# A hybrid decoder step on one core: the input projection with TensorE's order written out and the attention heads cut into smaller steps

## The chip, the cores and the metric

One core of a Trainium2 chip runs the whole kernel as one program. The metric is the device time of one execution in microseconds (us). TensorE (PE in the profile), VectorE (DVE), ScalarE (ACT), GpSimd (POOL) and the queue that issues most transfers (SP) work at the same time and wait for each other through semaphores. Each of them takes its instructions in the order that was laid down when the kernel was built.

## The reference, cut to what matters

```python
h = rms_norm(x, norm_mix_pre)                  # 1024 prompt rows + 8 sample rows, width 1024
rq, rk, rv, rg, dq, dk, dv = split(h @ w_in)   # 28 column blocks of 128
ro = retention_prompt(rq, rk, rv)              # 4 retention heads, chunks of 128 rows
# 4 differential heads; per block of 128 query rows and map m = 0, 1:
s[m] = dq[m] @ dk[m].T * 64**-0.5 + alibi      # causal
p[m] = softmax(s[m])
do = (p[0] - lam * p[1]) @ dv
# the 8 sample rows attend to 1024 cached keys each: 64 key pages and 64 value pages of 128 x 512
x = x + rms_norm(concat(retention_out(ro, rg), subnorm(do)) @ w_o)
x = x + rms_norm(conv_ffn(rms_norm(x)))        # gated MLP, width 2816
```

Everything is float32. The large products are made from three float32r products of high and low parts (`prod3`).

## The kernel before, in words

**Blocks.** The input projection makes 28 column blocks of 128 outputs, each transposed, in three segments of 344 of the 1032 rows. A segment is 24 products (8 slices of the width, three products each, L114 to L116), and a block is 72. VectorE scales each finished segment out of PSUM (`z_evac`, L220), and splits the next block's weights into high and low (L109, after ScalarE's L108). Blocks 20 and 24 are made in front of the loop; the loop then walks `blocks_left`, numbered n = 0 to 25: first block 16, then nine more blocks for the differential heads (e >= 16), then sixteen for the retention heads.

**Side work.** Three generators are advanced from inside this loop, one `next` at a time, and each `yield` ends one step. `sides` runs the four differential heads and then the four retention heads. `credit` grows by a rate after every segment, and each whole credit runs one step: `D_RATE` 1.42 while differential blocks are made, `R_RATE` 0.88 afterwards. A third generator, `sample_attention`, starts behind block 19 and is paced by `K_PACE` 3.0 and `V_PACE` 2.35 steps a segment: one step takes one cached page. A key page is multiplied on GpSimd (L493) and summed on VectorE (L484); of the value pages every second one goes to GpSimd (L577, L579), the others to VectorE (L584, L586). Pages have four buffers (`PG_BUFS`).

**A differential head** (`diff_head`) splits its queries and keys into high and low parts and moves halves between partitions by nine transfers on SP's queue (L324 to L332), loads the position bias, and turns its values by 8 transposes. For each of 8 blocks of 128 query rows ("rows" below, i = 0 to 7, width 128(i+1)) it makes scores for two maps (L345, L346), adds the bias and finds the minimum on VectorE (L348), takes the exponential on ScalarE (L400), joins the two maps on VectorE (L408, L409), transposes the joined weights (`tr`, L292), copies them on ScalarE (L357) and multiplies them with the values (`av_mm`, L366). `tr` and `av_mm` of row i come while row i+2 is being scored. A float32 product such as L366 is issued as two instructions. The weights live in eight buffers shared by all such tiles (`aux`).

**What sets the order.** A planner orders every engine's instructions when the kernel is built, by its own costs, with the order of the program as priority. It may put a head's products far in front of block products that stand earlier in the program. Only in the MLP (`fixed`) is TensorE held to the order of the program.

Of the kernel before, what the change touches and what calls it, by code (L numbers as in the profile page):

```python
# [9 lines left out]
F32 = mybir.dt.float32  # L10
# [3 lines left out]
ALU = mybir.AluOpType  # L14
# [31 lines left out]
D_RATE, R_RATE, K_PACE, V_PACE = 1.42, 0.88, 3.0, 2.35  # L46
# [5 lines left out]
def step_kernel(ctx: ExitStack, tc: tile.TileContext, gam, g128, xT, w_in, w_o, w_f, w_y, norms, ngb, cst, subln,  # L52
# [257 lines left out]
    def diff_head(h):  # L310
        zq, zk, zv = Z.pop(16 + h), Z.pop(20 + h), Z.pop(24 + h)
# [7 lines left out]
        ql = zq[:, 0:T].bitcast(F32R)  # L319
        nc.scalar.activation(qs[0], zq[:, 0:T], AF.Copy)  # L320
        nc.scalar.activation(ks[0], zk[:, 0:T], AF.Copy)
        nc.vector.tensor_tensor(ql, zq[:, 0:T], qs[0].bitcast(F32), ALU.subtract)
        nc.vector.tensor_tensor(kl[0], zk[:, 0:T], ks[0].bitcast(F32), ALU.subtract)
        nc.sync.dma_start(ks[1][lo_h].bitcast(F32), ks[0][hi_h].bitcast(F32))  # L324
        nc.sync.dma_start(ks[1][hi_h].bitcast(F32), ks[0][hi_h].bitcast(F32))
        nc.sync.dma_start(qs[1][hi_h].bitcast(F32), qs[0][hi_h].bitcast(F32))
        nc.sync.dma_start(qs[1][lo_h].bitcast(F32), ql[hi_h].bitcast(F32))
        nc.sync.dma_start(ks[0][hi_h].bitcast(F32), ks[0][lo_h].bitcast(F32))
        nc.sync.dma_start(qs[0][hi_h].bitcast(F32), ql[lo_h].bitcast(F32))
        nc.sync.dma_start(kl[1][lo_h].bitcast(F32), kl[0][hi_h].bitcast(F32))  # L330
        nc.sync.dma_start(kl[1][hi_h].bitcast(F32), kl[0][hi_h].bitcast(F32))
        nc.sync.dma_start(kl[0][hi_h].bitcast(F32), kl[0][lo_h].bitcast(F32))  # L332
# [3 lines left out]
        yield  # L336
# [4 lines left out]
        def score(i, m, n0, w, pt, mn):  # L341
            n1 = min(w, n0 + 512)
            sps = bank("S", "sps")[:, 0:n1 - n0]
            q = slice(i * P, (i + 1) * P)
            nc.tensor.matmul(sps, lhsT=qs[m][:, q], rhs=ks[m][:, n0:n1], start=True, stop=False)  # L345
            nc.tensor.matmul(sps, lhsT=qs[m][:, q], rhs=kl[m][:, n0:n1], start=False, stop=True)  # L346
            mo = pa.tile([P, 1], F32, tag="mn", bufs=6, name="mn")
            nc.vector.tensor_tensor_reduce(pt[:, n0:n1], sps, bias[:, 1024 - w + n0:1024 - w + n1],  # L348
                                           -1.0, mn, ALU.add, ALU.min, mo)
            return mo  # L350
# [30 lines left out]
        on0 = None  # L381
        mt = m_out("mtd")
        for i in range(8):
            w = (i + 1) * P
            if i > 1:
                tr(i - 2)
# [16 lines left out]
            p0, p1 = pm_  # L403
# [7 lines left out]
            yield  # L411
            if i == 6:
                post2(0, on0)
        tr(6)
        av_mm(6)
        yield
        tr(7)
        av_mm(7)
        on1 = post1(1)
        yield  # L420
        yield
        post2(1, on1)
# [180 lines left out]
    def ret_head(h):  # L603
# [8 lines left out]
        for g in range(2):  # L612
            aps = bank4("S", "aps")
            for i in range(4):
# [3 lines left out]
                                    ALU.mult)  # L618

        for g in range(2):  # L620
            transpose4(blocks(zv, g), lambda tp: nc.scalar.activation(vn[:, 4 * g:4 * g + 4, :], tp, AF.Copy))
        yield
        for g in range(2):
            transpose4(blocks(zk, g), lambda tp: nc.scalar.activation(
                kn[:, 4 * g:4 * g + 4, :], tp, AF.Identity, scale=ct[:, C_KD + h:C_KD + h + 1]))
        nc.gpsimd.tensor_tensor(qd, qd, rd[:, 1:2, :].broadcast_to([P, 8, P]), ALU.mult)
        yield
        st = aux([P, 8, P], name="st")
        for g in range(2):
# [4 lines left out]
            for i in range(4):  # L634
# [3 lines left out]
                else:  # L638
                    nc.vector.scalar_tensor_tensor(st[:, c, :], st[:, c - 1, :], g128[h], kvp[:, i, :],
                                                   ALU.mult, ALU.add)  # L640
        nc.scalar.dma_start(rsp[h], st[:, 7, :])
# [766 lines left out]
```

## Time and profile before

| | |
|---|---|
| median of 3 runs | 1392.24 us (1391.69 to 1393.86) |
| the profiled execution: time, span | 1392.55 us, 1390.8 us |
| PE busy | 1316.7 us (95%) |
| DVE busy | 977.7 us (70%) |
| ACT busy | 573.9 us (41%) |
| POOL busy | 491.7 us (35%) |
| mean granted clock of TensorE | 0.987 of 2.4 GHz |

The time of an execution is 1.75 us more than the span, which runs from the first to the last instruction. Busy times are shares of the span. A matmul's busy time is modelled and overlaps with the next one's, so a stretch in which products follow each other closely shows as fully busy; how fast products really go is read from the distance between their starts.

### The profile page before, as it was taken

How to read it: one execution, taken by the hardware profiler on the slowest of the kernel's cores; microseconds unless marked ns; L12 is line 12 of the kernel's file. 1: busy time of each engine (PE TensorE's matmuls, PEld its weight loads, DVE VectorE, ACT ScalarE, POOL GpSimd, SP SyncE). 2: the span in 40 equal slices, each digit the busy share in tenths (PEclk: the TensorE clock that was granted, in tenths of full speed). 3: DMA queues.
4: the chain of work that ended last, by engine and by line, in shares of the span. 5: the costliest groups of instructions: out<-in, count | busy, mean ns of one | idle time of the engine just before them, and what ended most of it. 6: DMA issues, size and time to landing. Idle time of an engine off the chain costs nothing.

```text
span 1390.8 us, 22794 instructions
## 1 busy us (share of the span) xinstructions
PE 1316.7 (95%) x8235; PEld 1269.2 (91%) x8235; DVE 977.7 (70%) x1773; ACT 573.9 (41%) x1148; POOL 491.7 (35%) x402
## 2 busy tenths in 40 slices
PE   6999989889999999996799999999999999989998
PEld 5999887878999998996799999999999999989976
DVE  6575759879678865477877777767777655576585
ACT  5254515235222144343444434344444435546544
POOL 5300456745546621438523313323323100050130
PEclk9999999999999999998999999999999999999999
DMA  5434285764554534231122222221221268668675
GB/s 220 127 101 126 86 245 185 214 205 125 164 192 144 176 111 160 90 127 52 68 76 77 94 87 71 82 82 65 83 81 66 95 224 270 214 210 260 198 237 161
DMA packets 98355, 196.51 MB, mean 141 GB/s; under 512 B 17595, under 2 KB 47419, under 8 KB 98243
## 3 DMA queue, kind: packets, MB, share of 16 engines
q1 hardware_dynamic: 91378, 183.45, 41.6%
q10 hardware_dynamic: 6864, 11.62, 2.3%
q8 instruction: 64, 1.05, 0.3%
q14 instruction: 49, 0.39, 0.1%
HBM read 155.11 MB, written 30.48 MB: 133 GB/s over the span
## 4 chain that ended last, share of the span: by engine, by line
PE 64%; DVE 15%; POOL 7%; DMA 6%; issue 5%; ACT 2%; SPq 1%; POOLq 0%; DVEq 0%; ACTq 0%
PE ps_in L114 4%; PE ps_in L115 4%; PE ps_in L116 4%; PE ps_y L1218 3%; PE ps_y L1217 3%; PE ps_y L1219 3%; DVE acc_v L586 3%; PE pb L1023 3%; PE pb L1024 3%; PE pb L1022 3%; PE gp L1022 2%; PE up L1024 2%; PE pc L1023 2%; PE pc L1024 2%; PE up L1023 2%
## 5 line engine op out<-in xcount | busy, mean ns | idle before, releaser
L114 PE MATMUL ps_in<-xh,wh 128*128 128x344 f32 x672 | 223.6, 333 | 8.0 <-ACT xh L192 6.1
L115 PE MATMUL ps_in<-xl,wh 128*128 128x344 f32 x672 | 220.1, 328 | 2.1 <-DVE xl L193 2.1
L116 PE MATMUL ps_in<-xh,wl 128*128 128x344 f32 x672 | 218.6, 325 | 1.0 <-DVE wl L109 1.0
L114 PEld LDWEIGHTS ps_in<-xh,wh 128*128 128x128 f32 x672 | 129.0, 192 | 11.4 <-ACT xh L192 6.1
L160 POOL TENSOR_TENSOR acc<-acc,sq 128x344 f32<-128x344 f32 (+1 forms) x56 | 61.3, 1095 | 205.6 <-ACT sq L159 201.0
L115 PEld LDWEIGHTS ps_in<-xl,wh 128*128 128x128 f32 x672 | 128.9, 192 | 4.8 <-DVE xl L193 3.8
L1158 DVE TENSOR_TENSOR wyl<-wyraw,wyh 128x1024 fp32r<-128x1024 f32 x66 | 84.4, 1279 | 67.0 <-ACT wyh L1157 64.7
L116 PEld LDWEIGHTS ps_in<-xh,wl 128*128 128x128 f32 x672 | 128.9, 192 | 1.5 <-DVE wl L109 1.3
L1041 POOL TENSOR_TENSOR S<-wraw 128x512 f32<-128x512 f32 x20 | 30.8, 1541 | 266.5 <-DMA wraw<-in_w_f 239.3
L1218 PE MATMUL ps_y<-al,wyh 128*128 128x388 f32 x352 | 119.4, 339 | 2.4 <-DVE al L1169 2.4
L1219 PE MATMUL ps_y<-ah,wyl 128*128 128x388 f32 x352 | 119.1, 338 | 1.2 <-DVE wyl L1158 1.2
L1217 PE MATMUL ps_y<-ah,wyh 128*128 128x388 f32 x352 | 119.7, 340 | 0.3 <-ACT wyh L1157 0.3
L493 POOL TENSOR_TENSOR pg<-pg,qb 128x512 f32<-128x512 f32 x64 | 90.6, 1434 | 40.7 <-DMA pg<-in_kpool 26.6
L1157 ACT ACTIVATE wyh<-wyraw 128x1024 fp32r<-128x1024 f32 x66 | 69.7, 1056 | 59.5 <-PE ps_y L1218 33.1
L990 DVE TENSOR_TENSOR ww<-S,ww 128x512 fp32r<-128x512 f32 x80 | 85.4, 1086 | 8.4 <-ACT ww L989 8.4
L990 DVE TENSOR_TENSOR ww<-wraw,ww 128x512 fp32r<-128x512 f32 x80 | 74.8, 935 | 21.5 <-ACT ww L989 19.8
L989 ACT ACTIVATE ww<-wraw 128x512 fp32r<-128x512 f32 x80 | 50.2, 628 | 95.8 <-PE up L1024 65.5
L989 ACT ACTIVATE ww<-S 128x512 fp32r<-128x512 f32 x80 | 50.5, 634 | 94.1 <-POOL S L1042 35.0
L1169 DVE TENSOR_TENSOR al<-ar,ah 128x388 fp32r<-128x388 f32 (+2 forms) x110 | 62.5, 578 | 25.5 <-ACT ah L1168 24.7
L108 ACT ACTIVATE wh<-wraw 128x1024 fp32r<-128x1024 f32 (+1 forms) x41 | 42.5, 1036 | 83.3 <-PE ps_in L115 38.6
L1023 PE MATMUL pb<-tw,ww 128*128 128x344 f32 x240 | 76.8, 320 | 0.0
L1024 PE MATMUL pb<-tw,ww 128*128 128x344 f32 x240 | 76.8, 320 | 0.0
(324 smaller groups left out, 3877.6 us busy)
## 6 DMA issues: line engine op xcount, KB each, us to landing
wyraw<-in_w_y SPq DMA_DIRECT2D x66, 512.0 KB, 4.0
wraw<-in_w_f SPq DMA_DIRECT2D x44, 512.0 KB, 3.3
pg<-in_kpool SPq DMA_DIRECT2D x64, 256.0 KB, 3.0
pg<-in_vpool SPq DMA_DIRECT2D x64, 256.0 KB, 2.8
wraw<-in_w_in SPq DMA_DIRECT2D x27, 512.0 KB, 4.2
ar<-ad SPq DMA_DIRECT2D x44, 194.0 KB, 3.9
ad<-cc SPq DMA_DIRECT2D x20, 344.0 KB, 2.2
ar<-ad SPq DMA_DIRECT2D x44, 150.0 KB, 3.4
```

What stands on the lines that cost most here:

```text
L114: nc.tensor.matmul(ps, lhsT=wh[:, k, :], rhs=ah[:, k, n0:n1], start=(first and i == 0), stop=False)
L115: nc.tensor.matmul(ps, lhsT=wh[:, k, :], rhs=al[:, k, n0:n1], start=False, stop=False)
L116: nc.tensor.matmul(ps, lhsT=wl[:, k, :], rhs=ah[:, k, n0:n1], start=False, stop=(last and i == len(order) - 1))
L493: nc.gpsimd.tensor_tensor(kp, kp, qb.rearrange("p (a b) -> p a b", b=P), ALU.mult)
L989: nc.scalar.activation(hi, t, AF.Copy)
L990: nc.vector.tensor_tensor(lo, t, hi.bitcast(F32), ALU.subtract)
L1023: nc.tensor.matmul(ps, lhsT=w[:, 0, k], rhs=bl, start=False, stop=False, skip_group_check=True)
L1024: nc.tensor.matmul(ps, lhsT=w[:, 1, k], rhs=bh, start=False, stop=(last and k == 3), skip_group_check=True)
L1158: nc.vector.tensor_tensor(wl, raw, wh.bitcast(F32), ALU.subtract)
L1217: nc.tensor.matmul(pss[d], lhsT=wh[:, i, w], rhs=ah, start=(f == 0), stop=False)
L1218: nc.tensor.matmul(pss[d], lhsT=wh[:, i, w], rhs=al, start=False, stop=False)
L1219: nc.tensor.matmul(pss[d], lhsT=wl[:, i, w], rhs=ah, start=False, stop=(f == NF - 1))
```

## The change

From n = 1 on, TensorE's instructions keep the order of the program (`inorder`, closed behind the loop). Each segment's 24 products are cut into pieces of 9, 9 and 6, and side work is advanced (`tick`) behind each piece and not only behind each segment: nine times a block. The rates are given anew for the finer beat, with a third one, `E_RATE`, for retention blocks made while a differential head still runs. A differential head now yields after each map's scores, after each row's value products and after each row's transposes; value products come three rows behind the scores, a row further than their transposes' two. The splitting of a head's queries and keys (`diff_prep`) is taken out and run for the next head behind the current one's last scores. Retention heads yield in the middle of their first steps. Blocks 22 and 26 are made in front of block 19, so that sample attention, which starts behind block 19, starts at n = 7 and not at n = 5.

```diff
-D_RATE, R_RATE, K_PACE, V_PACE = 1.42, 0.88, 3.0, 2.35
+D_RATE, E_RATE, R_RATE, K_PACE, V_PACE = 1.6, 0.85, 0.55, 1.1, 0.85
...
+    def diff_prep(h):
+        zq, zk = Z.pop(16 + h), Z.pop(20 + h)
...
     def diff_head(h):
+        if h not in ready:
+            diff_prep(h)
+            for _ in range(16):
+                yield
+        ks, qs, kl, bias = ready.pop(h)
+        zv = Z.pop(24 + h)
         vn = zv[:, 0:T].rearrange("p (a b) -> p a b", b=P)
         for g in range(2):
             transpose4(blocks(zv, g), lambda tp: nc.scalar.activation(vn[:, 4 * g:4 * g + 4, :], tp, AF.Copy))
-        yield
+            yield
...
+        def done_row(i):
+            av_mm(i)
+            return post1(i // 4) if i % 4 == 3 else None
...
         for i in range(8):
             w = (i + 1) * P
-            if i > 1:
-                tr(i - 2)
...
             for m in range(2):
                 pt = aux([P, 1024], name="pt")
-                mn = score(i, m, 0, w, pt, 3e38)
-                if m == 1 and i > 1:
-                    av_mm(i - 2)
-                    if i == 5:
-                        on0 = post1(0)
-                if w > 512:
-                    mn = score(i, m, 512, w, pt, mn)
+                mn = score(i, m, w, pt)
                 nc.scalar.activation(pt[:, 0:w], pt[:, 0:w], AF.Exp, bias=mn, scale=-1.0,
                                      accum_out=sm[:, m:m + 1])
                 pm_.append(pt)
+                yield
+                if m == 0:
+                    if i > 2:
+                        on = done_row(i - 3) or on
+                        yield
+                    if i > 1:
+                        tr(i - 2)
+                        yield
...
+        if h < H - 1 and have(17 + h, 21 + h):
+            diff_prep(h + 1)
+        av_mm(5)
+        yield
+        tr(6)
+        yield
+        post2(0, on)
+        yield
+        tr(7)
+        yield
+        av_mm(6)
+        yield
+        on = done_row(7)
+        for _ in range(4):
             yield
...
-    blocks_left = [16, 17, 21, 25, 18, 19, 22, 26, 23, 27] + \
+    blocks_left = [16, 17, 21, 25, 18, 22, 26, 19, 23, 27] + \
         [e for h in range(H) for e in (4 + h, h, 8 + h, 12 + h)]
...
+    def tick(e):
+
+        nonlocal credit, pages_due
+        credit += D_RATE if e >= 16 else (E_RATE if "pool" not in PR else R_RATE)
+        while credit >= 1.0:
+            next(side, None)
+            credit -= 1.0
+        if "pager" in PR:
+            pages_due += V_PACE if "v" in PR else K_PACE
...
+    inorder = tc.manual_schedule(engines={mybir.EngineType.PE})
     for n, e in enumerate(blocks_left):
+        if n == 1:
+            inorder.__enter__()
...
-            z_unit(e, s, w, ps)
+            for ks in ((0, 1, 2), (3, 4, 5), (6, 7)):
+                prod3(ps, *w, *xhl[s], ks, 0, SEG, first=(ks[0] == 0), last=(ks[-1] == ND - 1))
+                if ks[-1] < ND - 1 and n:
+                    tick(e)
...
-            if done >= 3:
-                credit += D_RATE if e >= 16 else R_RATE
-                while credit >= 1.0:
-                    next(side, None)
-                    credit -= 1.0
+            if n:
+                tick(e)
             if e == 19 and s == 2:
                 PR["pager"] = sample_attention()
...
+    closed(inorder)
```

## Rows read from the trace of the kernel before

**Rows 1.** Busy time of each engine in stretches of the input stage; columns in the first line.

```profile
core 0: us, PE busy (x) PEld busy (x) DVE busy (x) ACT busy (x) POOL busy (x), PEclk, DMA share, GB/s
58.30:157.00 98.70, 98.59 (x651) 93.24 (x651) 61.18 (x183) 47.97 (x118) 4.17 (x9) 1.00 0.38 106
157.00:304.00 147.00, 132.07 (x836) 122.02 (x835) 117.75 (x240) 50.89 (x119) 95.27 (x73) 0.99 0.67 201
304.00:322.00 18.00, 16.96 (x114) 15.75 (x112) 14.13 (x50) 11.50 (x27) 2.17 (x4) 1.00 0.56 176
322.00:503.00 181.00, 174.66 (x1290) 167.64 (x1290) 147.04 (x291) 43.86 (x115) 102.41 (x86) 0.99 0.49 156
503.00:518.70 15.70, 15.70 (x112) 15.64 (x111) 8.70 (x13) 6.88 (x9) 2.58 (x2) 1.00 0.45 140
...
58.30:518.70 460.40, 437.98 (x2994) 414.28 (x2994) 348.79 (x774) 161.10 (x387) 206.60 (x172) 0.99 0.53 160
```

**Rows 2.** The same stretches, products of L114 alone (24 make a block).

```profile
0.00:58.30 58.30, 25.49 (x73) 15.52 (x73) 0.97 0.47 172
...
157.00:304.00 147.00, 58.77 (x180) 33.84 (x180) 0.99 0.67 201
```

**Rows 3.** TensorE in order of time: start, length, engine, line, count, [wait].

```profile
92.81 0.34 PE L345 MATMUL sps<-ks,qs 128*128 128x384 f32 x1
92.99 0.34 PE L346 MATMUL sps<-kl,qs 128*128 128x384 f32 x1
93.16 0.32 PE L116 MATMUL ps_in<-xh,wl 128*128 128x344 f32 x1
...
360.45 1.95 PE L616 MATMUL aps<-z 128*128 128x128 f32 x16
362.23 1.04 PE L292 MATMUL tp<-ct,z 128*128 128x128 f32 x8
363.03 0.40 PE L114 MATMUL ps_in<-xh,wh 128*128 128x344 f32 x1
363.27 0.32 PE L115 MATMUL ps_in<-xl,wh 128*128 128x344 f32 x1
363.42 0.32 PE L116 MATMUL ps_in<-xh,wl 128*128 128x344 f32 x1
363.58 0.32 PE L114 MATMUL ps_in<-xh,wh 128*128 128x344 f32 x1
```

**Rows 4.** All engines in order of time around one wait of TensorE.

```profile
249.43 3.49 POOL L493 TENSOR_TENSOR pg<-pg,qb 128x512 f32<-128x512 f32 x2 [0.17 <-DMA pg<-in_kpool]
...
249.80 1.99 DVE L409 SCALAR_TENSOR_TENSOR pt<-pt,cf 128x1024 f32<-128x1024 f32 x1
...
249.86 0.32 PE L115 MATMUL ps_in<-xl,wh 128*128 128x344 f32 x1
...
251.93 1.06 PE L292 MATMUL tp<-ct,pt 128*128 128x128 f32 x8 [1.76 <-DVE pt L409]
```

**Rows 5.** VectorE from 80 to 140 us, by shape: count, busy, mean ns.

```profile
L348 DVE CUSTOM_DVE_ANT_0 pt<-sps,bias 128x512 f32<-128x512 f32 x12 | 8.1, 684 | 0.6 <-PE sps L346 0.4 <-PE tp L292 0.2
...
L408 DVE SCALAR_TENSOR_TENSOR cf<-sm,nlam,rs 128x1 f32<-128x1 f32 x12 | 2.5, 209 | 0.0
...
L409 DVE SCALAR_TENSOR_TENSOR pt<-pt,cf 128x1024 f32<-128x1024 f32 x1 | 1.3, 1274 | 0.0
```

**Rows 6.** VectorE from 190 to 310 us, by shape.

```profile
L408 DVE SCALAR_TENSOR_TENSOR cf<-sm,nlam,rs 128x1 f32<-128x1 f32 x12 | 8.9, 738 | 0.0
L348 DVE CUSTOM_DVE_ANT_0 pt<-sps,bias 128x512 f32<-128x512 f32 x12 | 8.1, 677 | 0.0
L109 DVE TENSOR_TENSOR wl<-wraw,wh 128x1024 fp32r<-128x1024 f32 x6 | 8.0, 1336 | 0.0
...
L409 DVE SCALAR_TENSOR_TENSOR pt<-pt,cf 128x1024 f32<-128x1024 f32 x1 | 2.0, 1989 | 0.0
```

**Rows 7.** ScalarE from 190 to 310 us, by shape.

```profile
L400 ACT ACTIVATE pt<-pt,mn 128x1024 f32<-128x1024 f32 x2 | 2.3, 1152 | 1.0 <-DVE mn L348 1.0
```

**Rows 8.** Costliest groups of the whole run, the sample pages on GpSimd.

```profile
L493 POOL TENSOR_TENSOR pg<-pg,qb 128x512 f32<-128x512 f32 x64 | 90.6, 1434 | 40.7 <-DMA pg<-in_kpool 26.6 <-DMA qb<-q8d 6.7 <-DVE on L371 3.6
...
L579 POOL TENSOR_TENSOR acc_v<-acc_v,pg 128x512 f32<-128x512 f32 x28 | 38.0, 1356 | 2.1
...
L577 POOL TENSOR_TENSOR pg<-pg,at 128x512 f32<-128x512 f32 x28 | 35.0, 1250 | 33.9 <-DMA pg<-in_vpool 23.9 <-DVE acc_v L586 7.9 <-DVE z L220 1.8
```

**Rows 9.** SP's queue, 150 to 320 us: waiter, awaited, us in total, times, longest.

```profile
SPq L462 <- DVE sc L484: 40.2, 27, 4.0
```

**Rows 10.** The chain that ended last, pieces around the second and third head's start.

```profile
196.07 4.29 DMA ks<-ks
...
269.48 6.07 DMA qs<-qs
275.56 3.25 DMA qs<-z
```

More of the change, by code (lines that the diff above doesn't have):

```diff
@@ L326, in diff_head, with have @@
         nc.sync.dma_start(qs[1][hi_h].bitcast(F32), qs[0][hi_h].bitcast(F32))
+        nc.sync.dma_start(kl[1][lo_h].bitcast(F32), kl[0][hi_h].bitcast(F32))
+        nc.sync.dma_start(kl[1][hi_h].bitcast(F32), kl[0][hi_h].bitcast(F32))
         nc.sync.dma_start(qs[1][lo_h].bitcast(F32), ql[hi_h].bitcast(F32))
         nc.sync.dma_start(ks[0][hi_h].bitcast(F32), ks[0][lo_h].bitcast(F32))
+        nc.sync.dma_start(kl[0][hi_h].bitcast(F32), kl[0][lo_h].bitcast(F32))
         nc.sync.dma_start(qs[0][hi_h].bitcast(F32), ql[lo_h].bitcast(F32))
-        nc.sync.dma_start(kl[1][lo_h].bitcast(F32), kl[0][hi_h].bitcast(F32))
-        nc.sync.dma_start(kl[1][hi_h].bitcast(F32), kl[0][hi_h].bitcast(F32))
-        nc.sync.dma_start(kl[0][hi_h].bitcast(F32), kl[0][lo_h].bitcast(F32))
+        ready[h] = (ks, qs, kl, bias)
+    def have(*es):
+        return all((e, 2) in seen for e in es)
+    def diff_head(h):
+        if h not in ready:
[4 more added lines that the diff above has]
+        zv = Z.pop(24 + h)
         vn = zv[:, 0:T].rearrange("p (a b) -> p a b", b=P)
@@ L339, in diff_head, with score @@
         OP = {}
[L341 to L350, printed above, removed]
+        def score(i, m, w, pt):
+            mn = 3e38
+            for n0 in range(0, w, 512):
+                n1 = min(w, n0 + 512)
+                sps = bank("S", "sps")[:, 0:n1 - n0]
+                q = slice(i * P, (i + 1) * P)
+                nc.tensor.matmul(sps, lhsT=qs[m][:, q], rhs=ks[m][:, n0:n1], start=True, stop=False)
+                nc.tensor.matmul(sps, lhsT=qs[m][:, q], rhs=kl[m][:, n0:n1], start=False, stop=True)
+                mo = pa.tile([P, 1], F32, tag="mn", bufs=6, name="mn")
+                nc.vector.tensor_tensor_reduce(pt[:, n0:n1], sps, bias[:, 1024 - w + n0:1024 - w + n1],
+                                               -1.0, mn, ALU.add, ALU.min, mo)
+                mn = mo
+            return mn
         def tr(i):
@@ L723, in sides @@
         for h in range(H):
-            while not all((e, 2) in seen for e in (16 + h, 20 + h, 24 + h)):
+            while not have(16 + h, 20 + h, 24 + h):
                 yield
@@ L744, in step_kernel @@
     credit = pages_due = 0.0
-    blocks_left = [16, 17, 21, 25, 18, 19, 22, 26, 23, 27] + \
+    blocks_left = [16, 17, 21, 25, 18, 22, 26, 19, 23, 27] + \
         [e for h in range(H) for e in (4 + h, h, 8 + h, 12 + h)]
-    done = 2
+    def tick(e):
[6 more added lines that the diff above has]
+            pages_due += V_PACE if "v" in PR else K_PACE
+            while pages_due >= 1:
+                pages_due -= 1
+                if next(PR["pager"], 0) == 0:
+                    del PR["pager"]
+                    break
+    inorder = tc.manual_schedule(engines={mybir.EngineType.PE})
     for n, e in enumerate(blocks_left):
+        if n == 1:
+            inorder.__enter__()
         w = w_next
```

32 lines of the change are left out of this document (9 added, 23 removed).

## The prediction

> **What bounds the kernel now.** I read the page first: TensorE is busy 95% of the span, so this change, which takes no product away, can win only what TensorE loses where the change acts. I then cut the input stage into stretches. The loop behind its first block starts at 58.3 us, by when 73 products of L114, three blocks of 24, are issued [rows 2]; its last product is issued before 518.7. In these 460.4 us TensorE shows 22.4 us without a product, and nearly all lie in two stretches [rows 1]: 14.9 us from 157 to 304, where key pages run beside differential heads, and 6.3 us from 322 to 503, where value pages run beside retention heads. Before 157, with no pages, it loses 0.1 us. Where pages run, VectorE is busy 80% and 81% and GpSimd 65% and 57%: no engine is full, but each waits for another in a fixed order. [rows 4] show it in small: eight transposes wait 1.76 us for the joined weights (L409) that VectorE finishes late, and block products whose inputs are ready stand behind them on TensorE.
>
> **What TensorE's work costs.** Busy times hide part of the loss, so I price the stage by distances between starts [rows 3]. A block product takes 0.158 us (363.27 to 363.58, two of them). The 16 instructions of L616 take 1.78 us, 0.111 each. Eight transposes take 0.80, 0.10 each. The first block product behind a float32 group takes 0.24, so each return costs 0.08 more. Two score products of 384 columns take 0.35, 0.46 ns a column.
>
> - 25 blocks: 25 x 72 x 0.158 = 284.
> - A differential head: 72 instructions of L366 at 0.111 = 8.0; 36 + 8 + 8 transposes = 5.2; 18,432 score columns = 8.4; some 24 returns = 1.9; together 23.5, four heads 94.
> - A retention head: 62 instructions at 0.111 = 6.9, 24 transposes 2.4, small products and returns about 2.7 (an estimate from their number, at 0.03 to 0.11 each): 12; with 3.25 heads inside the loop, 39.
> - Sample attention: 8 + 16 + 8 + 72 small products, about 7.
> - The clock: the mean granted clock is 0.99 in two stretches [rows 1], so 0.01 x 328 = 3.
>
> Sum 427 of 460.4: some 33 us can be had at most, 22.4 of them seen as gaps.
>
> **The change, part by part.**
>
> *The order.* No instruction comes or goes. A wait on TensorE now stands where the program puts it. What decides is whether each product's input is done in time. The steps are counted from the code: a differential block gives 9 x 1.6 = 14.4 steps, a head takes 39 (3 or 4 a row, two for its values, 10 at its end), the first head 16 more. So head 0's rows begin at n = 2, head 1 runs n = 4.7 to 7.4, head 2 n = 7.4 to 10.4. Head 3 gets 9 x 0.85 = 7.65 a block and ends at n = 15.6. Retention heads, 15 steps each, then get 4.95 a block; head 3 of these starts at n = 24.7 and leaves 11 of 15 steps behind the loop, against 6 of 8 before. So the work behind 518.7 is nearly the same, and I take it at nothing; its cover is the seven eighths of four output products placed there.
>
> *Distance.* `tr` of a row stands six or seven steps behind that row's last scores: 6.5 / 1.6 = 4 pieces of 1.27 us mean, 5.1 us, beside some 3.5 us of the row's own products. The chain in it for the widest row is two L348 at 0.68, the exponential at 1.15 [rows 7], L408 at 0.21 and L409 at 1.27 without GpSimd's work [rows 5]: 4.0, with some small operations and the passing on about 5 us. Covered. With L409 at 1.99 and L408 at 0.74 [rows 6] it is some 6.5 us plus what stands ahead of it on VectorE: covered with 2 us to spare. At the end of a head `tr(7)` is only four steps behind: there I expect up to 2 us a head for heads 2 and 3.
>
> *Value products a row later.* No cost on an engine; a weights tile is held a row longer, and with bias and one key part all eight buffers are then in use. If transposes are late, VectorE's next L348 waits for a buffer and the scores behind it wait for their bank.
>
> *Preparation earlier.* The nine transfers and the bias load are the same, now issued ten steps and a head's tail ahead of the first scores: 6 pieces and about 8 us of products, some 16 us. Before, landings of 4.29, 6.07 and 3.25 us stood in the chain [rows 10]. On SP's queue they stand behind page loads that wait for a free buffer, 40.2 us in 27 waits [rows 9]; for head 3 alone, the one prepared beside pages, this can eat the lead. I take 0 to 3 us.
>
> *Pages.* They start at the end of n = 7 (about 190 us, not 157) and run 9.9 and 7.65 steps a block, not 9 and 7.05. The 64 key pages and the eight steps behind them must fit into 6.4 blocks.
>
> *The sum, by stretches.* Blocks n = 1 to 7: 80 for blocks, 47 for two heads, 1 for head 2's beginning: 128; without pages TensorE lost almost nothing before [rows 1], so 132. Key pages, n = 8 to 14.4: 73 for blocks and 1.85 heads at 23.5 = 43, with a little of the samples: 118. VectorE's need there is what it is now, 117.75 us for 7.5 blocks [rows 1, 2], less one block's 2.8 (three L220, one L109): 115. Two engines with 118 and 115 us cannot both be kept full: at today's 90% of TensorE (132.07 of 147) the stretch takes 131, with all waits gone 118. I take 126, as the distances are larger than those of [rows 4]. The rest, n = 14.4 to 25: 132 for blocks, 4 for head 3's end, 39, 6: 181; today TensorE is busy 96.5% there, so 187. With the clock's 2: 132 + 126 + 187 + 2 = 447 against 460.4, 13.4 us less. From the profiled execution's 1392.55, which is 0.31 above the median, this gives **1379 us**.
>
> **The shared path of VectorE and GpSimd.** L409 on 1024 columns takes 1274 ns while GpSimd is quiet and 1989 while it works on pages; L408, one column wide, 209 and 738; L348, one operand of which is in PSUM, does not change, 684 and 677 [rows 5, 6]. So VectorE's operations on two tensors in SBUF stand still while GpSimd works. Denser pages would make that worse, which is the first rival. The Trainium skill, "SBUF — State Buffer", section "SBUF: two separate sides", says that these two engines share one pair of ports as an exclusive lock held for the whole instruction, the other blocking fully; the trace agrees, with 209 against 738 ns. By it the two engines' times add up, as the first rival works out from rows.
>
> **Rivals.**
>
> 1. *No gain: GpSimd and VectorE's two-tensor work can't overlap.* In the key pages' stretch GpSimd is busy 95.3 us [rows 1]; VectorE's two-tensor work is about 15 L409 at a mean of 0.8 (an estimate from 1.27 at full width), 7 L109 at some 1.2, 15 L408 at 0.21 and two preparations at 2.4: 28. Sum 123, fitting 147 easily but 126 at 98%. At 90% the stretch takes 137, and VectorE's part of the value pages adds some 3: 11 + 3 us worse than my sum, **1393**. For it: the inflated rows. Against: GpSimd still idles 40.7 us before key pages, 26.6 of it for their landing [rows 8]. Chance 0.15.
> 2. *Slower: the pages become a chain of their own.* If pages keep today's rate (147 us, 18 between, 181) while starting at 190 instead of 157, they end at 536, and the loop, which holds the last page sum's product at n = 25, ends near 540: **1414**. Mechanism: page buffers come free through VectorE, SP waits 40.2 us for that [rows 9], and in-order TensorE then waits for the page sums. It decides when pages take more than 323 us instead of today's 346, which would end the loop where it ends now. Against: GpSimd's own need is 64 x 1.43 and 32 x 2.61 us [rows 8], 175 us of 323. Chance 0.15.
> 3. *All waits gone.* The stage falls to its need, 427 of 460.4: **1361**; for it, the 0.1 us lost where no pages run. Chance 0.2.
>
> **How the numbers follow.** My forecast has 0.5, its own range 1370 to 1387. The median of three can tell 0.2%, 2.8 us, from no change. Faster: all of my forecast and of the third rival, a little of the first: 0.71. Same: most of the first and a pager slightly late: 0.12. Slower: 0.17. The range reaches from all waits gone to a third of the second rival's loss: 1361 to 1399; the second rival's full price stays outside.
>
> **What would show it.** Right: the last block product of the loop starts near 505, not 518; key pages start near 190 and end near 316; TensorE's idle time in that stretch falls to some 8 us and its waits for L409 vanish; preparation no longer stands in the chain. Wrong: key pages take 140 us or more (first rival, if L408 and L409 grow beyond 738 and 1989 ns), the last value sums come after 515 with TensorE waiting for them (second), or waits of block products for L220, which now can't be filled by other products.

## The result and the profile after

The changed kernel takes **1423.49 us** (1421.74 to 1425.06, 4 runs) against 1391.97 for the kernel before in the same comparison (4 runs): ratio 1.0239, interval 1.0205 to 1.0273. It is 31.5 us slower, where 13 us faster was forecast; 1423 lies outside the range of 1361 to 1399, on the side that had a chance of 0.17.

In the changed kernel L361 and L362 are the score products (L345 and L346 before), L364 is the score evacuation (L348), L429 and L430 are the coefficient and the joined weights (L408, L409), L509 is the key page's sum on VectorE (L484), L518 its multiplication on GpSimd (L493), L611 the value page's sum on VectorE (L586), L726 a step in the retention head's end (L698). The page's head with the core's mean granted clock, then the stretches of the input loop, which answer to [rows 1]: n = 1 to 7, key pages, the rest of the loop, and the work behind it up to the next stage.

```profile
span 1419.6 us, 22785 instructions
...
PE 1324.6 (93%) x8235; PEld 1285.1 (91%) x8235; DVE 977.9 (69%) x1773; ACT 583.1 (41%) x1152; POOL 484.3 (34%) x402
...
core 0: 1419.6 us, clock 0.971
```

```profile
core 0: us, PE busy (x) PEld busy (x) DVE busy (x) ACT busy (x) POOL busy (x), PEclk, DMA share, GB/s
59.60:190.20 130.60, 127.39 (x864) 123.72 (x863) 77.32 (x218) 62.19 (x148) 6.30 (x11) 1.00 0.44 120
190.20:332.50 142.30, 125.05 (x775) 119.57 (x773) 114.34 (x254) 59.79 (x128) 90.38 (x74) 0.93 0.60 180
332.50:544.00 211.50, 190.29 (x1361) 183.22 (x1360) 153.99 (x302) 48.49 (x118) 105.62 (x88) 0.94 0.48 155
544.00:663.60 119.60, 109.08 (x704) 104.62 (x703) 69.56 (x131) 51.81 (x112) 38.13 (x37) 0.97 0.36 117
```

VectorE, ScalarE and GpSimd are busy within 2% of what they were. The loop's last product starts at 544.0, not 518.3; behind it the next stage's first product comes 119.6 us later, where the kernel before took 117.1. So 25.7 of the 28.8 us by which the span grew have come up by the loop's end. Without pages (first line) little is lost: TensorE stands 3.2 of 130.6 us; 132 were forecast. Beside key pages TensorE stands 17.3 us (142.3 less 125.05), beside value pages 21.2, and its mean granted clock falls to 0.93 and 0.94, where it was 0.99.

What TensorE waited for, beside key pages (190 to 352 us) and beside value pages (352 to 544), by waiter and awaited (us in total, times, longest):

```profile
PE sps L361 <- DVE mn L364: 9.7, 4, 4.4
PE tp L292 <- DVE pt L430: 5.5, 2, 4.2
PE st_ps L534 <- DVE sc L509: 2.6, 2, 2.4
...
PE tp L292 <- DVE m L726: 14.1, 3, 8.4
```

These are on VectorE, few and long: in the kernel before, no wait of TensorE in the loop was longer than 2.1 us. The longest, 8.41 us, in order of time, VectorE first and then TensorE:

```profile
457.78 0.16 DVE L304 TENSOR_SCALAR ss<-ss 128x4 f32<-128x4 f32 x1
459.07 1.53 DVE L307 TENSOR_TENSOR att<-att,rrn 128x512 f32<-128x512 f32 x1 [1.13 <-POOL rrn L306]
460.52 2.30 DVE L109 TENSOR_TENSOR wl<-wraw,wh 128x1024 fp32r<-128x1024 f32 x1
462.75 4.04 DVE L611 SCALAR_TENSOR_TENSOR acc_v<-pg,at,acc_v 128x128 f32<-128x128 f32 x8
466.71 0.15 DVE L304 TENSOR_SCALAR ss<-ss 128x4 f32<-128x4 f32 x1
468.00 1.53 DVE L307 TENSOR_TENSOR att<-att,rrn 128x512 f32<-128x512 f32 x1 [1.13 <-POOL rrn L306]
...
469.88 0.15 DVE L726 TENSOR_SCALAR m<-t 128x8 f32<-128x8 f32 x1
```

```profile
457.54 0.29 PE L724 MATMUL t<-sm,ct 128*128 128x8 f32 x2
...
461.07 0.60 PE L292 MATMUL tp<-ct,att 128*128 128x128 f32 x4
470.08 1.11 PE L292 MATMUL tp<-ct,att 128*128 128x128 f32 x4 [8.41 <-DVE m L726]
```

L726 takes 0.15 us and its input was there by 457.8. It starts 12 us later, because VectorE's queue holds a weight block's L109, eight value sums and the normalization of `att` ahead of it, which itself goes by GpSimd (1.13 us). The profile names L726 because it ended last, but it decides only half a microsecond: the four transposes at 470.08 also read the second half of `att`, whose normalization is L304, L306 on GpSimd and L307, and this L307 ends at 469.53. ScalarE had the squares for L304 ready by 457.4; L304, of 0.15 us too, starts 9 us later, behind the first half's L307, L109 and the value sums. At the changed kernel's two other waits for L726 it is the same: that L307 ends half a microsecond before. So its "waits for L726" are waits for this chain on VectorE. The block products that could fill the 8.41 us stand behind the transposes in TensorE's fixed order; but the planner's order, below, leaves a wait of 8.3 us at the same transposes. What such a wait costs beyond itself shows in TensorE's windows around it (length, busy, granted clock):

```profile
460.00:462.00 2.00, 1.67 (x12) 1.00 0.30 97
462.00:464.00 2.00, 0.00 (x0) 0.91 0.48 137
464.00:466.00 2.00, 0.00 (x0) 0.50 0.84 242
...
470.00:472.00 2.00, 1.92 (x8) 0.50 0.44 100
472.00:474.00 2.00, 2.00 (x9) 0.53 0.90 338
474.00:476.00 2.00, 2.00 (x17) 1.00 0.70 280
```

The clock falls to the 1.2 GHz level two us into the wait, and the first 3.8 us of products behind it run there: 9 products in 2 us, then 17. The loop holds seven such stretches, 44.4 us in all, in 31.8 of which TensorE works; in the kernel before it was two, 6.8 us.

### The profile page after: what moved, and what is told of

It is laid out like the page before. It is cut to its first block, busy times and chain, and to the rows that moved or that the text cites. A ratio compares the mean times of both kernels' runs of the same rounds, so it can differ in the third digit from the quotient of the medians.

```text
span 1419.6 us, 22785 instructions
## 1 busy us (share of the span) xinstructions
PE 1324.6 (93%) x8235; PEld 1285.1 (91%) x8235; DVE 977.9 (69%) x1773; ACT 583.1 (41%) x1152; POOL 484.3 (34%) x402
## 4 chain that ended last, share of the span: by engine, by line
PE 67%; DVE 15%; POOL 7%; issue 5%; DMA 4%; ACT 2%; POOLq 0%; DVEq 0%; SPq 0%; ACTq 0%
PE ps_in L114 4%; PE ps_y L1256 4%; PE ps_y L1258 4%; PE ps_y L1257 4%; PE ps_in L116 4%; PE ps_in L115 4%; PE pb L1062 3%; PE pb L1063 3%; PE pb L1061 3%; DVE acc_v L611 2%; PE gp L1061 2%; PE up L1063 2%; PE pc L1062 2%; PE pc L1063 2%; PE up L1062 2%
## 5 line engine op out<-in xcount | busy, mean ns | idle before, releaser
L114 PE MATMUL ps_in<-xh,wh 128*128 128x344 f32 x672 | 233.7, 348 | 8.3 <-ACT xh L192 6.4
L115 PE MATMUL ps_in<-xl,wh 128*128 128x344 f32 x672 | 223.5, 333 | 1.8 <-DVE xl L193 1.8
L116 PE MATMUL ps_in<-xh,wl 128*128 128x344 f32 x672 | 222.8, 332 | 1.0 <-DVE wl L109 1.0
L114 PEld LDWEIGHTS ps_in<-xh,wh 128*128 128x128 f32 x672 | 133.8, 199 | 11.7 <-ACT xh L192 6.4
L115 PEld LDWEIGHTS ps_in<-xl,wh 128*128 128x128 f32 x672 | 133.7, 199 | 4.0 <-DVE xl L193 3.1
L116 PEld LDWEIGHTS ps_in<-xh,wl 128*128 128x128 f32 x672 | 133.1, 198 | 1.2 <-DVE wl L109 1.2
L518 POOL TENSOR_TENSOR pg<-pg,qb 128x512 f32<-128x512 f32 x64 | 86.4, 1372 | 31.8 <-DMA pg<-in_kpool 21.9
L1029 DVE TENSOR_TENSOR ww<-wraw,ww 128x512 fp32r<-128x512 f32 x80 | 74.8, 936 | 21.2 <-ACT ww L1028 19.4
L413 ACT ACTIVATE pt<-pt,mn 128x128 f32<-128x128 f32 (+7 forms) x64 | 49.6, 775 | 80.0 <-DVE mn L364 79.6
L1062 PE MATMUL pb<-tw,ww 128*128 128x344 f32 x240 | 76.8, 320 | 0.0
```

Source lines behind the costliest of these rows:

```text
L114: nc.tensor.matmul(ps, lhsT=wh[:, k, :], rhs=ah[:, k, n0:n1], start=(first and i == 0), stop=False)
L115: nc.tensor.matmul(ps, lhsT=wh[:, k, :], rhs=al[:, k, n0:n1], start=False, stop=False)
L116: nc.tensor.matmul(ps, lhsT=wl[:, k, :], rhs=ah[:, k, n0:n1], start=False, stop=(last and i == len(order) - 1))
L518: nc.gpsimd.tensor_tensor(kp, kp, qb.rearrange("p (a b) -> p a b", b=P), ALU.mult)
L1029: nc.vector.tensor_tensor(lo, t, hi.bitcast(F32), ALU.subtract)
L1062: nc.tensor.matmul(ps, lhsT=w[:, 0, k], rhs=bl, start=False, stop=False, skip_group_check=True)
```

## The experiments

**Where the loss is made.** Two kernels start the whole of sample attention only behind the loop, the changed one and the kernel before. The pages then stand alone, so that the whole time (1568.9 and 1564.9 us, one run each) says nothing; the loop does.

```diff
-            if e == 19 and s == 2:
-                PR["pager"] = sample_attention()
...
+    PR["pager"] = sample_attention()
```

> The changed kernel with sample attention started behind the loop, so that no page runs beside heads; its 128 pages then run alone and the whole time grows by some 150 us or more, which says nothing: read is the loop's last product alone. Theories A and B both need pages for the loss: last product at 490 to 505 us against 544, waits of TensorE below 2 us each. If instead the distances written into the steps are too short even without pages (theory C), the loop still ends after 520 with waits of several us.

> The kernel before with sample attention started behind the loop; its time grows by some 150 us and says nothing, read is the loop's last product alone. In the changed kernel that product starts at 477.8 without pages. If the fixed order wins what it can where no page runs, the old order ends later here, at 488 to 500; if the two orders are worth the same without pages, 475 to 484.

The loop's last product starts at 477.8 (earlier than the 490 to 505 expected) and at 478.8. The changed kernel without pages:

```profile
58.30:478.00 419.70, 415.82 (x2880) 405.85 (x2879) 216.80 (x562) 167.09 (x382) 37.39 (x47) 1.00 0.31 92
```

So the need of 427 us was right to a few us: less the 7 of the samples and the 3 put for the clock, which stayed at 1.00 here, it is 417, and TensorE is busy for 415.8. Without pages the new order is worth 1 us, and all distances are long enough (longest wait 1.5 us). Pages add 40 us to the loop before (518.3 less 478.8 = 39.5) and 66 to the changed one.

**The order or the pages.** The planner's order given back to the changed kernel; the fixed order given to the kernel before; the pages of the changed kernel at their old place and rate; and the first and third together.

```diff
# planner_order: the changed kernel without these
-    inorder = tc.manual_schedule(engines={mybir.EngineType.PE})
-            inorder.__enter__()
-    closed(inorder)
# order_only: the kernel before with the same three lines
# pages_as_before: in the changed kernel
-D_RATE, E_RATE, R_RATE, K_PACE, V_PACE = 1.6, 0.85, 0.55, 1.1, 0.85
+D_RATE, E_RATE, R_RATE, K_PACE, V_PACE = 1.6, 0.85, 0.55, 1.0, 0.783
-    blocks_left = [16, 17, 21, 25, 18, 22, 26, 19, 23, 27] + \
+    blocks_left = [16, 17, 21, 25, 18, 19, 22, 26, 23, 27] + \
```

> The changed kernel with the planner's order for TensorE given back; finer steps, rates, value products a row later, early preparation and block order stay. Theory A (fixed order: VectorE's and GpSimd's lateness beside the pages is much as it was, but TensorE now waits for it with ready products behind the waiting one): 1385 to 1402 us, the loop's last product near 515 to 525, no single wait of TensorE over 3 us beside pages. Theory B (pages start two blocks later and run denser, so that VectorE and GpSimd need longer than TensorE): 1415 us or more, the loop's last product near 540, whoever sets TensorE's order.

> The kernel before with TensorE held to the order of the program from n = 1 on, and nothing else of the change: steps are whole rows, run behind segments. Theory A: slower than the kernel before by 25 us or more, as its distances are shorter than the changed kernel's (transposes and value products of a row follow each other directly). Theory B: 1385 to 1400 us, near the kernel before.

> The changed kernel with block 19 back in its old place and the page rates of before (9 and 7.05 steps a block, written as 1.0 and 0.783 a tick); the fixed order and all else stay. Theory B: 1385 to 1402 us, as pages again have two blocks more. Theory A: within 10 us of the changed kernel, 1413 to 1433, as VectorE is late beside pages at either pace.

> The changed kernel with the planner's order for TensorE, block 19 in its old place and the page rates of before: what is left of the change are finer steps, value products a row later and early preparation. Theory B (the later and denser pages are what costs 19 us under the planner's order): 1385 to 1398 us. If the finer steps themselves cost it: 1405 or more.

Measured: planner's order 1411.8 (ratio to the kernel before 1.0136, 1.0112 to 1.0159); order only 1425.6 (1.0228, 1.0201 to 1.0255); pages as before 1428.5 (1.0256, 1.0228 to 1.0284); both 1416.0 (1.0157, 1.0127 to 1.0188). Later and denser pages are not the cause: their old place helped neither kernel (4 to 5 us more, within overlapping intervals). The fixed order costs 11.7 us (1423.5 less 1411.8) and, with the pages at their old place, 12.5. On the kernel before it costs 33. Some 20 us remain with the planner's order, against both A's and B's numbers. A's other sign, no wait over 3 us, fails too: with the planner's order TensorE's largest waits in the loop are those of the changed kernel.

```profile
PE tp L292 <- DVE m L726: 14.1, 3, 8.3
PE sps L361 <- DVE mn L364: 8.8, 3, 5.1
```

So in the changed kernel the fixed order did not make the long waits, and the planner's order did not fill them. In the profiled executions the two loops end 8.4 us apart (544.0 and 535.6); 4.6 of this is idle time, 3.0 half clock.

**Which part of the change costs under the planner's order.** Five versions. `ticks_only` is the kernel before with blocks cut into pieces and rates divided by three; `new_diff_head_alone` is it with the new differential head alone; `old_ret_head` is the last version above (1416.0) with the retention head as it was, `old_diff_head` that version with the differential head as it was; `pages_early_thin` spreads the old kernel's pages over more blocks.

```diff
# ticks_only, against the kernel before
-D_RATE, R_RATE, K_PACE, V_PACE = 1.42, 0.88, 3.0, 2.35
+D_RATE, E_RATE, R_RATE, K_PACE, V_PACE = 0.473, 0.293, 0.293, 1.0, 0.783
# new_diff_head_alone, against the kernel before: diff_prep and diff_head of the changed kernel, and
+D_RATE, E_RATE, R_RATE, K_PACE, V_PACE = 4.8, 2.55, 0.88, 3.0, 2.35
# pages_early_thin, against the kernel before
+D_RATE, R_RATE, K_PACE, V_PACE = 1.7, 0.88, 2.7, 2.15
+    blocks_left = [16, 17, 18, 19, 21, 25, 22, 26, 23, 27] + \
```

> From the version with the planner's order and the pages at their old place (1416.0 us), the differential head is put back as it was: 12 coarse steps at 0.473 a piece, value products two rows behind, preparation at the head's start; portions of a block and the retention head's splits stay. If the head's new steps are what costs under the planner's order (theory H): 1392 to 1402, loop's last block product by 525. If the retention head's splits cost (theory R): 1408 or more, with the loss beside value pages left. If the portions of three products cost (theory T): 1408 or more, with the loss beside key pages left.

> From the same version (1416.0 us) the retention head alone is put back as it was: 8 coarse steps at 0.293 a piece, the four splits gone. H: 1410 to 1418, no gain beside key pages. R: 1395 to 1405, with TensorE's waits beside value pages (6.5 us at 397, 5.5 at 452) gone. T: 1410 to 1418.

> Both heads put back as they were, so that of the change only the portions of three products are left (nine ticks a block instead of three, the same steps a block), under the planner's order. H or R: the time of before within 5 us, 1388 to 1397. T: 1405 or more.

> The kernel before with the new differential head alone (value products a row later, 39 short steps, early preparation), taken at 4.8 steps a piece of a block, without portions and splits, under the planner's order. If the head's part is neutral or a gain by itself (it cost 3.6 us on top of the portions): 1384 to 1397. If its short distances or its extra held buffer cost: 1400 or more, with TensorE's loss beside key pages.

> The kernel before with the query blocks 18 and 19 taken third and fourth, so that the pages start some four blocks (46 us) earlier, and paced thinner (2.7 and 2.15 a piece instead of 3.0 and 2.35), differential heads at 1.7. If the loss of the loop is the load of VectorE and GpSimd beside heads, spreading the pages over more blocks wins some of the 40 us they cost: 1375 to 1388. If what costs is each page's own collision with a head's chain, wherever it lies: 1390 to 1400. If the early blocks starve the first head (its keys and values come two blocks later): above 1400, with TensorE's idle time before 120 us from the loop's start.

Measured ratios to the kernel before: ticks only 1.0076 (1.0049 to 1.0102), new differential head alone 1.0076 (1.0049 to 1.0103), old retention head 1.0102 (1.0064 to 1.0139), old differential head 1.0255 (1.0216 to 1.0295), pages early and thin 1.0096 (1.0059 to 1.0133). H's times were not met: with the old differential head the time rose, from 1416.0 to 1424.9. But the loop itself got 5.2 us shorter (to 530.9 from 536.1); what was lost lies behind it, where the next stage's first product comes 132.9 us later and not 124.0. Of R's price some 13 us are seen (1416.0 to 1402.9), and of these too a large part lies behind the loop (113.9 us to the next stage). T's 1405 was not reached, nor the 1397 that H and R allowed (1399.5). Spreading pages won nothing and lost 13; in the loop's first 120 us TensorE stood 7.9 us instead of 2.1, but pages run there too, so whether a first head that waits for its blocks is behind it stays open. Every single step away from the kernel before costs about 10 us, and the steps don't add up: that asked for a control. Both kernels with three rates 3% lower and nothing else:

```diff
# before_rates
-D_RATE, R_RATE, K_PACE, V_PACE = 1.42, 0.88, 3.0, 2.35
+D_RATE, R_RATE, K_PACE, V_PACE = 1.38, 0.88, 2.9, 2.28
# after_rates
-D_RATE, E_RATE, R_RATE, K_PACE, V_PACE = 1.6, 0.85, 0.55, 1.1, 0.85
+D_RATE, E_RATE, R_RATE, K_PACE, V_PACE = 1.55, 0.85, 0.55, 1.065, 0.825
```

> The kernel before with three of its rates 3% lower (differential steps 1.42 to 1.38 a piece, key pages 3.0 to 2.9, value pages 2.35 to 2.28), nothing else. Thinner pages and heads have more time, which by loads alone changes next to nothing: 1388 to 1396. If the kernel before stands at a narrow optimum, so that any other meeting of pages and heads costs: 1399 or more; then differences of some 10 us between versions here are no price of an edit.

> The kernel after with the same three rates 3% lower (1.6 to 1.55, 1.1 to 1.065, 0.85 to 0.825). If the 31 us are a steady cost of the fixed order beside pages: 1418 to 1429. If they are one unlucky meeting of pages and heads: a move of more than 8 us either way.

The kernel before slows to 1409.5 us, ratio 1.0106 (1.0066 to 1.0146): thinner pages and heads cost 15 us. The changed one stays at 1423.9, ratio 1.0222 (1.0183 to 1.0262): its loss is steady under this move. Where the 15 us went, TensorE's waits beside key pages and beside value pages in the kernel before with its rates lower:

```profile
PE tp L292 <- DVE on L307: 8.4, 1, 8.4
PE tp L292 <- DVE pt L409: 5.2, 2, 3.9
...
PE ps_in L114 <- ACT att L689: 6.1, 1, 6.1
PE tp L292 <- DVE m L698: 3.6, 1, 3.6
```

The same code, the same loads, and four waits of 3.6 to 8.4 us that weren't there at 1.42, 3.0 and 2.35. So the kernel before stands at a favourable meeting of pages and heads, and differences of some 10 us between versions here are no price of an edit. One direction and one size of the move were tried, not more.

**Which engine's work is behind the waits.** From the changed kernel: without GpSimd's 64 key multiplications (one run; the sample rows' scores are then not the reference's), without VectorE's 64 key sums (those scores are not formed at all), with VectorE in program order too, with the last transposes of a retention head three steps later, and with the retention head's steps as they were.

```diff
# no_key_multiply
-                nc.gpsimd.tensor_tensor(kp, kp, qb.rearrange("p (a b) -> p a b", b=P), ALU.mult)
# no_key_sum
-                if held:
-                    reduce_page(*held)
# dve_in_order
+    inorder = tc.manual_schedule(engines={mybir.EngineType.PE, mybir.EngineType.DVE})
# retention_tail: R_RATE 0.55 -> 0.66, and ahead of the last transposes
-        yield
+        for _ in range(4):
+            yield
# fixed_old_ret_head: the four added yields of ret_head out, R_RATE 0.55 -> 0.293
```

> The changed kernel without GpSimd's 64 multiplications of key pages, so that VectorE sums unmultiplied pages (the sample rows' scores are not those of the reference); transfers, sums and all else stay, and GpSimd is quiet in the stretch of the key pages. Theory C (GpSimd's work stops VectorE's two-tensor operations, and TensorE waits for those): L430 on 1024 columns and L429 fall to 1.27 and 0.21 us, the stretch from 190 us to the first value page at 352 shrinks from 162 to 145 or less. Theory D (VectorE's load and the page transfers alone): it stays at 152 or more.

> The kernel after without VectorE's 64 key page sums (L509; the sample rows' scores are then not formed); GpSimd's 64 multiplications stay. If VectorE's share is what delays the heads (K by VectorE's queue): 1400 or less, the scores' waits for L364 and the transposes' for L430 gone beside key pages. If GpSimd's hold on VectorE's two-tensor work is the cause (K by the shared path): 1412 to 1424, L429 still above 400 ns and L430 above 1000. The loss beside value pages stays by either.

> The kernel after with VectorE in program order as well as TensorE, over the same blocks. If TensorE waits because the planner puts page work (value sums, L109, page sums) ahead of a head's operation on VectorE's queue (theory Q): 1395 to 1412, with the waits of the retention transposes for L726 (14.1 us) and of the scores for L364 (9.7) at a third. If the load decides, whatever the order (theory K): 1417 to 1430. If VectorE in order then stands itself behind a page that GpSimd has not finished (12.3 us of its idle time in the key pages' stretch now) and holds up the scores: 1435 or more, with VectorE's idle time for L518 above 25 us.

> The changed kernel with three more steps between a retention head's last sums and its last transposes, and R_RATE 0.66 instead of 0.55, so that a head takes as many blocks. In the changed kernel these transposes wait 14.1 us in all for VectorE behind value pages. If TensorE's waits there are a matter of distance: those waits fall below 5 us and the time by 7 to 12 us, to 1411 to 1417. If VectorE is full there and the wait only moves on: 1420 to 1427.

> The kernel after, fixed order kept, with the retention head's steps put back as they were (8 coarse ones at 0.293 a tick). If the splits cost by themselves, as they did under the planner's order (7.7 us between two versions there): 1412 to 1418, the waits for L726 down by half or more. If under the fixed order only the distance behind VectorE counts (coarse steps give the last transposes about as many block products ahead as now): 1419 to 1428.

Without the multiplications the loop ends at 526.1 (18 us earlier; 1400.1 us), without the sums at 530.5 (13.5 earlier; 1408.7 us, ratio 1.0099, 1.0069 to 1.0129). The first mixes two things: the sums, no longer behind a multiplication, also ran earlier, so that only 5 of 64 stood in 190 to 334 us. The second is cleaner. The stretch from 190 us to the first value page shrinks from 162 us to 144 in the first, theory C's number, and to 148 in the second. VectorE's coefficient and joined weights beside key pages, without the multiplications, and then without the sums:

```profile
L430 DVE SCALAR_TENSOR_TENSOR pt<-pt,cf 128x1024 f32<-128x1024 f32 x2 | 2.6, 1284 | 0.1
...
L429 DVE SCALAR_TENSOR_TENSOR cf<-sm,nlam,rs 128x1 f32<-128x1 f32 x16 | 3.4, 210 | 0.0
```

```profile
L429 DVE SCALAR_TENSOR_TENSOR cf<-sm,nlam,rs 128x1 f32<-128x1 f32 x16 | 10.2, 634 | 0.0
L430 DVE SCALAR_TENSOR_TENSOR pt<-pt,cf 128x768 f32<-128x768 f32 x2 | 4.0, 1988 | 0.1
...
L430 DVE SCALAR_TENSOR_TENSOR pt<-pt,cf 128x512 f32<-128x512 f32 x2 | 2.0, 992 | 0.0
```

210 ns without GpSimd's work and 634 with it, 1284 ns for 1024 columns without and 1988 for 768 with: the hold of GpSimd is real, and stays when VectorE's load is gone. The transposes' waits for L430 are gone without the sums. The scores' waits for L364 stay at 9.7 us without the sums and are gone without the multiplications, and the loop wins 13.5 and 18: the numbers named for the second run (1400 or less; 1412 or more) were not met, and the two engines each bear part of it.

VectorE in program order is worse, 1455.4 us (1.045, 1.0418 to 1.0481). Its waits beside key pages:

```profile
PE sps L361 <- DVE mn L364: 23.1, 9, 8.3
PE ps_in L114 <- DVE z L220: 6.6, 3, 5.4
PE st_ps L534 <- DVE sc L509: 3.5, 3, 2.6
```

Theory Q falls: the planner's order of VectorE is the better one. The time is that of the third case; its sign is not, as VectorE's wait for L518 was 12.4 us, not above 25.

Three more steps ahead of the last retention transposes give 1411.3 (1.012, 1.0082 to 1.0157), 12 us, as expected of distance: the waits for L726 fall from 14.1 to 2.3 us. One for L307 of 6.1 takes their place: it is the wait of 8.41 us above, now shorter, and named by the second half of `att`. The old steps of that head give 1409.8 (1.0111, 1.0078 to 1.0145), better than either theory: the waits for L726's counterpart fall from 14.1 to 5.2, but the loop ends only 2.5 us earlier (541.5), and 9.3 of the gain lie behind it (110.3 us up to the next stage, not 119.6), as some 30 of TensorE's instructions that stood behind the loop are now inside it. The retention head's splits, with the rate that goes with them, cost 13.1 us under the planner (1416.0 less 1402.9) and 13.7 in the fixed order; with the control's 15 us in mind, two pairs that agree make this likely, not certain. No version beat the kernel before.

## Why the prediction was wrong

The loop of ten versions side by side: from 58.3 us to its last product (in the first two to 478.0 and 518.7), TensorE's idle time in it, the time in which it works at half clock (busy time within the stretches of granted clock 0.5), and its longest wait.

| version | loop, us | idle, us | busy at half clock, us | longest wait, us |
|---|---|---|---|---|
| without pages (changed kernel) | 419.7 | 3.9 | 0 | 1.5 |
| before | 460.4 | 22.4 | 6.8 | 2.1 |
| ticks only | 466.3 | 24.6 | 16.6 | 3.4 |
| before, rates 3% lower | 479.5 | 35.4 | 23.8 | 8.4 |
| new differential head alone | 479.8 | 33.4 | 27.3 | 5.3 |
| changed, planner's order | 477.3 | 37.1 | 25.9 | 8.3 |
| changed, retention tail | 477.4 | 35.5 | 28.5 | 6.1 |
| changed, old retention head | 483.2 | 38.9 | 29.3 | 5.1 |
| changed | 485.7 | 41.7 | 31.8 | 8.4 |
| changed, VectorE in order | 519.2 | 68.7 | 40.3 | 8.3 |

Against the loop without pages the changed one is 66.0 us longer: 37.8 idle, 15.9 by the clock (half of 31.8), and 12 within time that shows as busy at full clock, in which also the samples' own products lie (7 by the prediction's estimate; the loop without pages has none). The loop before is 40.7 longer: 18.5, 3.4 and 19. So the change brought 19 us more of idle time, in longer waits, and behind them 12.5 more by the clock.

- **The need, 427 us, and n = 1 to 7, 132 us:** right to a few us (without pages 415.8 busy for 417; 130.6, though no reason stood for the 4 us by which 128 became 132). So were the start of key pages (the stretch begins at 190.2, the first multiplication at 199.8), the preparation (no wait of TensorE for one of its transfers is left in the loop), and the work behind the loop at nothing (119.6 for 117.1).
- **"Covered with 2 us to spare": the step that failed.** I summed the durations of `tr`'s own chain, with GpSimd's hold in them, and about one other operation ahead. I did not price VectorE's queue: two operations of 0.15 us stood 9 and 12 us behind others. At 80% busy [rows 1] VectorE was not full, but whatever comes due stands behind several page operations. And I worked the chain out for the widest row, and there it nearly held: the last row of head 2 waited 1.27 us, within the 2 I gave it, and head 3's widest row did not wait. The long wait for L430 stands at head 3's first and narrowest row, 128 columns. TensorE came to its transposes 7.5 us after the row's last scores (259.0 to 266.5), not much less than the distance I had priced; the chain took 11.6, though its operations are the shortest of the head. L364 started 3 us after the scores, behind page sums that waited for GpSimd, and the weights were joined 5 us after the exponential, behind page sums and a weight block.

```profile
261.70 0.69 DVE L509 TENSOR_REDUCE sc<-pg 128x8 f32<-128x512 f32 x1 [1.67 <-POOL pg L518]
262.30 0.28 DVE L364 CUSTOM_DVE_ANT_0 pt<-sps,bias 128x128 f32<-128x128 f32 x1
...
265.16 1.69 DVE L109 TENSOR_TENSOR wl<-wraw,wh 128x1024 fp32r<-128x1024 f32 x1
...
269.57 1.01 DVE L430 SCALAR_TENSOR_TENSOR pt<-pt,cf 128x128 f32<-128x128 f32 x1
...
270.72 0.45 PE L292 MATMUL tp<-ct,pt 128*128 128x128 f32 x1 [4.18 <-DVE pt L430]
```

I also put at nothing the score banks (9.7 us of waits for L364), which I had named, and the end of a retention head (14.1 for L726), where the rate that goes with the new splits (0.55 steps a piece, 0.293 before) brings product and transpose closer: I took that head as unchanged beside value pages. These two are the larger part.
- **The key pages' stretch, 126 us:** the same 6.4 blocks took 137, up to 327.6 instead of 316; the last key multiplication started at 332.5, after 6.7 blocks. I weighed 118 (no waits) against 131 (today's share) and chose between them "as the distances are larger"; a share below today's was not among the bounds, though I had taken from TensorE the freedom to put other products into a wait. I also let the key stretch end after 6.4 blocks, 64 pages at 9.9 a block; with the eight steps behind them value pages start after (64 + 8) / 9.9 = 7.3, at 352.7 us.
- **The rest, 187 us at "today 96.5%":** 216.4 (327.6 to 544.0). The head that I had not priced stands here.
- **The clock, 2 us:** 15.9. I took today's 0.99 over; the versions with longer waits than the kernel before all have more time at half clock.
- **The sum:** by the stretches shown above 130.6 + 142.3 + 211.5 = 484.4 where 447 stood, 37 us; the rest of the 43 (1422.39, the profiled execution, less 1379) is the 2.5 behind the loop, 1.3 at its start, and 2 outside.
- **The first rival** names key pages of 140 us or more as its sign, and by the stretch above (142.3) they came; but its condition didn't: L429 fell to 442 ns and L430 was 1277 at 1024 columns, no more than without GpSimd (other widths were held: 1628 ns at 640 columns, 884 without). The Trainium skill, "SBUF — State Buffer", section "SBUF: two separate sides", has VectorE's operations with two inputs in SBUF and GpSimd's block each other fully; the 210 and 634 ns above agree. By it alone the time would have been the 1393 of that rival.
- **The second rival** has nearly the size (1414, loop to 540) and not the mechanism. Its times came: the last value sum starts at 518.7, after 515, and the last product that reads these sums at 535.3. But no wait of TensorE in the loop is for a value sum, from the first multiplication (199.8) to the last value sum pages took 319 us where they took 324 before, and starting them earlier didn't help.
- **What I took as ground:** that 22 us of idle time in the kernel before are there to be won by a better order. The control says otherwise: at rates 3% lower the same kernel loses 13.0 us more in idle time (35.4 less 22.4) and 8.5 by the clock (half of 23.8 less 6.8). Of the 31 us, about 12 are the fixed order's, twice measured. For the other 20 the likeliest reading is that they are what leaving that meeting of pages and heads costs, and 13 of them go with the retention head's splits; this is argued, not shown. How these 20 are shared among the parts stays open, as a 3% move of rates is as large.

## What to carry to other kernels

Before a tuned interleaving is replaced, move its rates by a few per cent: if that costs as much as the gain that is hoped for, the idle time in its profile is no reserve, and single edits can't be priced on it below that size. A distance in program order must cover what the awaited engine's queue holds ahead of the awaited operation, not that operation's duration; read it from the queue's densest stretch, for every head that the stage runs, not for the one that the change is about. The widest piece of work is not the worst case for that: the chain that was priced here waited longest at its narrowest row. Fixing one engine's order while another's stays planned cost 12 us in two pairs here and won nothing, though the long waits were the same under either order. In the table, idle time orders the loops better than the longest wait does; the half clock behind the waits comes on top of it.

## What was not expected of the hardware

A longer wait need not be followed by more work at half clock. In the kernel before with its rates lower, transposes wait 3.87 us for L409; the windows that follow:

```profile
256.42 1.94 PE L292 MATMUL tp<-ct,pt 128*128 128x128 f32 x8 [3.87 <-DVE pt L409]
```

```profile
254.00:256.00 2.00, 0.00 (x0) 0.84 0.49 146
256.00:258.00 2.00, 1.58 (x8) 0.50 0.84 220
...
260.00:262.00 2.00, 2.00 (x12) 0.50 0.90 278
262.00:264.00 2.00, 2.00 (x14) 0.95 0.77 258
```

Behind this wait 5.8 us of work run at the 1.2 GHz level, behind the one of 8.41 us only 3.8. Here the clock was down for 7 us and only the first of them fell into the wait; there it was down for 10 us and 6 of them fell into the wait. These are two waits, no rule. And L429, on one column per partition, takes 210 ns in the mean without GpSimd's multiplications and 442 with them: an operation that moves one column can be held by that engine too.
